# Input table of a state space branch with its powers and products in PSUM, and the output table issued beside it

## The chip, the cores and the metric

The kernel runs on one core of one Trainium2 chip. The core has a matrix engine (TensorE, PE in the profile), VectorE (DVE), ScalarE (ACT), GpSimd (POOL), and DMA queues that SyncE (SP) issues. Each engine takes its instructions in the order of the program and waits for the others by semaphores. SBUF is the working memory; PSUM has eight banks of 2 KB per partition, in which TensorE leaves its products. The metric is the device time of one execution in microseconds.

## The reference, cut to what matters

One layer of an encoder with two branches; the change is in branch A, a bidirectional state space layer with 32 groups of 64 complex states.

```python
def _s5_branch(u, lam_re, lam_im, log_step, b_re, b_im, c_re, c_im, d_skip):
    ...
        ab_re = mag * jnp.cos(li * dt)
        ab_im = mag * jnp.sin(li * dt)
        ...
        bu_re = jnp.einsum('blgh,gph->blgp', ug, bb_re)
        bu_im = jnp.einsum('blgh,gph->blgp', ug, bb_im)
        ...
        _, _, s_re, s_im = lax.associative_scan(
            _cplx_scan_combine, (a_re, a_im, bu_re, bu_im), reverse=(direction == 1), axis=1)
        y = (y + jnp.einsum('blgp,ghp->blgh', s_re, c_re[direction].astype(f32))
             - jnp.einsum('blgp,ghp->blgh', s_im, c_im[direction].astype(f32)))
```

## The kernel before, in words

The sequence is cut into chunks of 8 positions. Powers 0 to 8 of the complex state factor (`pw`, made by `s5_params`) turn the branch into matrix products. An input table E (powers `pwE` times the input weights `Bb`) takes the 8 positions of a chunk to the state that the chunk adds; the products land in `X`. A scan over 64 chunk steps carries the state on, in place in `X`. An output table F (powers `pwF` times the output weights `Cc`) takes the carried state back to 8 positions; it is stored to DRAM (`fbscr`), and small kernels made of it (`kdscr`) are the part inside a chunk.

Both tables are made in 8 banks of 4 groups by `gbank`, six 128x512 operations a bank: on VectorE for E (`neg` false), on GpSimd for F (`neg` true). The rest of the stage is written as lanes, generators whose steps are issued at due times on a hand-kept clock of TensorE work: `e_lane` (E bank, its transposes on TensorE, the products with the input `Vt`, three copies to `X`, the last by VectorE), `scan_lane` ("r", 64 steps of three VectorE operations), `table_lane` ("s": F bank b, ScalarE's copies for it, TensorE's products of bank b-1 with `bm`, and for bank b-2 a VectorE addition to `ks` and the stores), `decay_params` ("d", VectorE), `ret_tables` ("x") and `y_lane` ("y", which reads both tables back and needs the whole scan). Between them run the plain projections (`kq_unit`, `v_unit`), whose weights are split into a high part `whi` by ScalarE and a low part `wlo` by VectorE.

The due times before start the table lane at 12 with a step of 5.4; the e lane runs from 0 to 12 and the scan starts at 13. Outside `gbank` the PSUM tiles are two-bank `pair` tiles (two of them) and one-bank `single` tiles (four of them). `late_params`, called near the end of the e lane, takes a `single` for the scan's factors (`A8`) and fills `pwF`.

An instruction that waits holds back all that stands behind it on its engine; so a `wlo` or a copy to `X` on VectorE stands behind whatever bank or scan step was issued before it. SP issues all DMAs in one order too: the store of F bank b-1 stands behind the `kdscr` stores of bank b-2, of which one waits for VectorE's addition to `ks`.

Of the kernel before, what the change touches and what calls it, by code (L numbers as in the profile page):

```python
# [8 lines left out]
F32 = mybir.dt.float32  # L9
# [42 lines left out]
R_T = (13, 0.997)  # L52
D_T = (15, 0.629)
X_T = (45, 1.361)
S_T = (12, 5.4)
T_FREE = 82.607
C_DT = 2.446
Y_T = (73, 3.91)
# [3 lines left out]
def build(nc, tc, I, O):  # L62
# [73 lines left out]
    def pair():  # L136
        return pp.tile([128, 2, 512], F32, name="pair", tag="pair")

    def single():
        return p1.tile([128, 512], F32, name="single", tag="single")  # L140
# [238 lines left out]
    prm = sp.tile([128, 3, G], F32, name="prm")  # L379
    Bb = sp.tile([128, 2, G, 16], F32, name="Bb")  # L380
    Cc = sp.tile([128, 2, G, 16], F32, name="Cc")
    pwE = sp.tile([128, 2, 8, G], F32, name="pwE")
    pwF = sp.tile([128, 2, 9, G], F32, name="pwF")
    Dg = sp.tile([48, 16, G], F32, name="Dg")

# [33 lines left out]
    def together(*gens):  # L419
        gens = list(gens)  # L420
        while gens:
            for g in list(gens):
                if next(g, gens) is gens:
                    gens.remove(g)
                else:
                    yield
# [4 lines left out]
            yield  # L431

    pw = sp.tile([128, 2, 9, G], F32, name="pw")
    sc = A8 = None

    def s5_params():
        V.memset(pw[:, 0, 0, :], 1.0)
        V.memset(pw[:, 1, 0, :], 0.0)
        dt = tmp()
        V.tensor_copy(out=dt, in_=prm[:, 2, :])  # L440
        yield
        yield from pexp(dt, G)
        lr, li = prm[:, 0, :], prm[:, 1, :]
        mag, den, dn = tmp(), tmp(), tmp()
        sc = []

        def magnitude():
            tt(V, mag, lr, dt, MUL)
            yield
            yield from pexp(mag, G)  # L450

        def angle():
            th, k1, kf, r, zz = tmp(), tmp(), tmp(), tmp(), tmp()
            c1 = 6.28125
            c2 = 0.0019340515136718750
            c3 = 2 * math.pi - c1 - c2
            yield from chain(
                lambda: tt(V, th, li, dt, MUL),
                lambda: ts(V, k1, th, 1.0 / (2 * math.pi), MUL, MAGIC, ADD),
                lambda: ts(V, kf, k1, -MAGIC, ADD),  # L460
                lambda: stt(r, kf, -c1, th, MUL, ADD),
                lambda: stt(r, kf, -c2, r, MUL, ADD),
                lambda: stt(r, kf, -c3, r, MUL, ADD),
                lambda: ts(V, r, r, 0.25, MUL),
                lambda: tt(V, zz, r, r, MUL))
            sn, cs = tmp(), tmp()

            def sine():
                ts(V, sn, zz, 1.0 / 362880, MUL)
                yield  # L470
                for c in (-1.0 / 5040, 1.0 / 120, -1.0 / 6):
                    stt(sn, sn, c, zz, ADD, MUL)
                    yield
                stt(sn, sn, 1.0, r, ADD, MUL)
                yield

            def cosine():
                ts(V, cs, zz, -1.0 / 3628800, MUL)
                yield
                for c in (1.0 / 40320, -1.0 / 720, 1.0 / 24, -0.5):  # L480
                    stt(cs, cs, c, zz, ADD, MUL)
                    yield
                ts(V, cs, cs, 1.0, ADD)
                yield

            yield from together(sine(), cosine())
            for _ in range(2):
                s2, c2t = tmp(), tmp()
                yield from chain(
                    lambda: tt(V, c2t, sn, sn, MUL),  # L490
                    lambda: stt(s2, sn, 2.0, cs, MUL, MUL),
                    lambda: ts(V, c2t, c2t, -2.0, MUL, 1.0, ADD))
                sn, cs = s2, c2t
            sc.extend((sn, cs))

        def denominator():
            yield from chain(
                lambda: tt(V, den, lr, lr, MUL),
                lambda: tt(V, dn, li, li, MUL),
                lambda: tt(V, den, den, dn, ADD),  # L500
                lambda: V.reciprocal(out=den, in_=den))

        yield from together(angle(), magnitude(), denominator())
        sn, cs = sc
        tt(V, pw[:, 0, 1, :], mag, cs, MUL)
        yield
        tt(V, pw[:, 1, 1, :], mag, sn, MUL)
        yield

        def powers():  # L510
            for st, n in ((1, 1), (2, 2), (4, 4)):
                ts_ = [x0.tile([128, 4, G], F32, name="pq", tag="pq", bufs=4)[:, :n] for _ in range(4)]
                ar = pw[:, 0, st:st + 1, :].to_broadcast([128, n, G])
                ai_ = pw[:, 1, st:st + 1, :].to_broadcast([128, n, G])
                xr, xi = pw[:, 0, 1:1 + n, :], pw[:, 1, 1:1 + n, :]
                for t, a, b in zip(ts_, (xr, xi, xr, xi), (ar, ai_, ai_, ar)):
                    tt(V, t, a, b, MUL)
                    yield
                tt(V, pw[:, 0, st + 1:st + 1 + n, :], ts_[0], ts_[1], SUB)
                yield  # L520
                tt(V, pw[:, 1, st + 1:st + 1 + n, :], ts_[2], ts_[3], ADD)
                yield

        bts = [x0.tile([128, G, 16], F32, name="bt", tag="bt", bufs=2) for _ in range(2)]

        def inputs():
            t1, t2, t3, t4, cr, ci, nr = (tmp() for _ in range(7))
            ai = pw[:, 1, 1, :]
            yield from chain(
                lambda: ts(V, nr, pw[:, 0, 1, :], -1.0, ADD),  # L530
                lambda: tt(V, t2, ai, li, MUL),
                lambda: tt(V, t3, ai, lr, MUL),
                lambda: tt(V, t1, nr, lr, MUL),
                lambda: tt(V, t4, nr, li, MUL),
                lambda: tt(V, t1, t1, t2, ADD),
                lambda: tt(V, t3, t3, t4, SUB),
                lambda: tt(V, cr, t1, den, MUL),
                lambda: tt(V, ci, t3, den, MUL))
            crb = cr[:, :, None].to_broadcast([128, G, 16])
            cib = ci[:, :, None].to_broadcast([128, G, 16])  # L540
            br, bi = braw[:, 0], braw[:, 1]
            tt(P, Bb[:, 0], br, crb, MUL)
            tt(P, bts[0], bi, cib, MUL)
            tt(P, Bb[:, 0], Bb[:, 0], bts[0], SUB)
            tt(V, Bb[:, 1], bi, crb, MUL)
            yield
            tt(V, bts[1], br, cib, MUL)
            yield
            tt(V, Bb[:, 1], Bb[:, 1], bts[1], ADD)
            yield  # L550

        yield from together(inputs(), powers())
        for ri in range(2):
            V.tensor_copy(out=pwE[0:64, ri], in_=pw[0:64, ri, 7::-1, :])
            yield
            V.tensor_copy(out=pwE[64:128, ri], in_=pw[64:128, ri, 0:8, :])
            yield

    def late_params():
        nonlocal sc, A8  # L560
        sc = single()
        A8 = sc[:, 0:128].rearrange("p (k r g) -> p k r g", k=2, r=2)
        for ri in range(2):
            V.tensor_copy(out=A8[:, 0, ri, :], in_=pw[:, 0, 8, :])
            ts(V, A8[:, 1, ri, :], pw[:, 1, 8, :], 1.0 if ri == 0 else -1.0, MUL)
            V.tensor_copy(out=pwF[0:64, ri, 1:9], in_=pw[0:64, ri, 1:9, :])
            V.tensor_copy(out=pwF[64:128, ri, 1:9], in_=pw[64:128, ri, 8:0:-1, :])  # L567
        ts(P, Cc[:, 1], Cc[:, 1], -1.0, MUL)
        tt(P, Dg[32:48], eye[32:48, :, None].to_broadcast([16, 16, G]),
           dcol[32:48, None, :].to_broadcast([16, 16, G]), MUL)  # L570

    x0_cm = pool("x0")
    x0 = enter(x0_cm)
# [177 lines left out]
    BK = 4  # L751
    NB = G // BK

    def gbank(b, pwt, t0, Bm, neg):
        gs = slice(b * BK, (b + 1) * BK)
        er9 = s5t.tile([128, BK, 9, 16], F32, name="er", tag="er", bufs=2)
        ei9 = s5t.tile([128, BK, 9, 16], F32, name="ei", tag="ei", bufs=2)
        er, ei = er9[:, :, 1:9], ei9[:, :, 1:9]
        if neg:
            act(er9[:, :, 0], Bm[:, 0, gs], AF.Copy)  # L760
# [3 lines left out]
        pi = pwt[:, 1, t0:t0 + 8, gs].rearrange("p t g -> p g t")[:, :, :, None].to_broadcast(sh)  # L764
        br = Bm[:, 0, gs, None, :].to_broadcast(sh)
        bi = Bm[:, 1, gs, None, :].to_broadcast(sh)
        tm = s5.tile([128, BK, 8, 16], F32, name="tm", tag="tm", bufs=1)
        tn = s5t.tile([128, BK, 8, 16], F32, name="tn", tag="tn", bufs=1)
        e = P if neg else V
        tt(e, er, pr, br, MUL)  # L770
        tt(e, tm, pi, bi, MUL)
# [298 lines left out]
    def spread(name, t0, dt, n):  # L1070
        return [(t0 + dt * i, name) for i in range(n)]

    events = deque(sorted(
        spread("e", *E_T, 16) + spread("r", *R_T, 64) + spread("s", *S_T, 10) + spread("d", *D_T, 45) + spread("x", *X_T, 24)
        + [(T_FREE, "free")] + spread("c", T_FREE + 0.1, C_DT, 12) + spread("y", *Y_T, 12), key=lambda e: e[0]))

    def passed(t):
# [1379 lines left out]
```

## Time and profile before

| | |
|---|---|
| median of 3 runs | 1308.06 us (1307.3 to 1308.17) |
| profiled execution | 1307.5 us, its span 1305.7 us |
| TensorE busy in the span | 1214.7 us (93%) |
| VectorE busy | 957.6 us (73%) |
| ScalarE busy | 591.7 us (45%) |
| GpSimd busy | 648.4 us (50%) |

The span is what the profile's clock covers; the execution's own time is 1.8 us longer. Times below are from the start of the span. The stage of the change lies between 56 us (the first E bank) and 226 us (the first products of the y lane). "Busy" is time in which an engine had an instruction running; an idle time in brackets stands before the instruction that ended it, with what released it. A row of busy times by stretch names the engines in the order TensorE, its weight loads, VectorE, ScalarE, GpSimd, with their instructions in brackets.

### The profile page before, as it was taken

How to read it: one execution, taken by the hardware profiler on the slowest of the kernel's cores; microseconds unless marked ns; L12 is line 12 of the kernel's file. 1: busy time of each engine (PE TensorE's matmuls, PEld its weight loads, DVE VectorE, ACT ScalarE, POOL GpSimd, SP SyncE). 2: the span in 40 equal slices, each digit the busy share in tenths (PEclk: the TensorE clock that was granted, in tenths of full speed). 3: DMA queues.
4: the chain of work that ended last, by engine and by line, in shares of the span. 5: the costliest groups of instructions: out<-in, count | busy, mean ns of one | idle time of the engine just before them, and what ended most of it. 6: DMA issues, size and time to landing. Idle time of an engine off the chain costs nothing. (4 is left out here: it accounts for less than half of the span.)

```text
span 1305.7 us, 19189 instructions
## 1 busy us (share of the span) xinstructions
PE 1214.7 (93%) x6821; PEld 1142.3 (87%) x6821; DVE 957.6 (73%) x1590; ACT 591.7 (45%) x1238; POOL 648.4 (50%) x621
## 2 busy tenths in 40 slices
PE   7899788998899999987899998999999999999996
PEld 7789678998888989976899887999999999988884
DVE  6997998548877776889764349856656556799797
ACT  5264344544354444342433224444444444567564
POOL 4306570436676656377755117543443444474174
PEclk8899889999999999997999999999999999999998
DMA  6351446766455433322353601333331222524002
GB/s 245 79 111 46 140 135 184 179 187 185 153 170 173 136 125 133 111 81 91 122 155 87 213 11 49 122 105 96 99 105 65 65 73 73 202 97 147 15 1 96
DMA packets 74495, 152.18 MB, mean 117 GB/s; under 512 B 17808, under 2 KB 35344, under 8 KB 74400
## 3 DMA queue, kind: packets, MB, share of 16 engines
q1 hardware_dynamic: 74400, 150.97, 37.5%
q8 instruction: 53, 0.87, 0.3%
q14 instruction: 42, 0.34, 0.1%
HBM read 116.92 MB, written 34.01 MB: 116 GB/s over the span
## 5 line engine op out<-in xcount | busy, mean ns | idle before, releaser
L90 DVE TENSOR_TENSOR wlo<-wraw,whi 128x512 fp32r<-128x512 f32 x298 | 246.7, 836 | 104.9 <-ACT whi L102 104.0
L102 ACT ACTIVATE whi<-wraw 128x512 fp32r<-128x512 f32 x304 | 183.3, 623 | 59.1 <-POOL wraw L90 32.8
L90 POOL TENSOR_TENSOR wraw<-wraw 128x512 f32<-128x512 f32 x93 | 132.1, 1421 | 139.5 <-DVE wlo L90 92.8
L90 POOL TENSOR_TENSOR wraw<-wrax,wraw 128x512 f32<-128x512 f32 x38 | 51.0, 1343 | 72.2 <-DVE wlo L90 41.3
L84 PE MATMUL bank<-n1hi,wlo 128*128 128x384 f32 x192 | 66.0, 344 | 1.7 <-DVE wlo L90 1.7
L82 PE MATMUL bank<-n1hi,whi 128*128 128x384 f32 x192 | 67.4, 351 | 0.0
L83 PE MATMUL bank<-n1lo,whi 128*128 128x384 f32 x192 | 66.0, 344 | 0.0
L82 PE MATMUL pair<-n1hi,whi 128*128 128x384 f32 (+1 forms) x168 | 62.2, 370 | 3.0 <-ACT sgst L102 3.0
L102 ACT ACTIVATE q<-bank 128x384 f32<-128x384 f32 x80 | 38.1, 483 | 52.8 <-PE bank L84 48.7
L84 PE MATMUL pair<-n1hi,wlo 128*128 128x384 f32 (+1 forms) x168 | 59.7, 355 | 0.0
L83 PE MATMUL pair<-n1lo,whi 128*128 128x384 f32 (+1 forms) x168 | 59.6, 355 | 0.0
L90 DVE TENSOR_TENSOR wlo<-wrax,whi 128x512 fp32r<-128x512 f32 x50 | 43.8, 883 | 15.8 <-ACT whi L102 15.8
L2289 PE MATMUL acc<-whi,ahi 128*128 128x512 f32 x132 | 52.4, 397 | 0.6 <-DVE hres L90 0.6
L2289 PE MATMUL acc<-whi,alo 128*128 128x512 f32 x132 | 52.3, 396 | 0.0
L2289 PE MATMUL acc<-wlo,ahi 128*128 128x512 f32 x132 | 52.3, 396 | 0.0
L90 DVE TENSOR_TENSOR X<-X,single 128x128 f32<-128x128 f32 (+2 forms) x128 | 42.9, 335 | 4.4
L90 POOL TENSOR_TENSOR er<-pwF,Cc 128x512 f32<-128x512 f32 x8 | 8.9, 1111 | 74.0 <-DVE pwF L567 43.0
L83 PE MATMUL bank<-yTlo,whi 128*128 128x384 f32 x128 | 43.0, 336 | 1.5 <-DVE yTlo L90 1.5
L84 PE MATMUL bank<-yThi,wlo 128*128 128x384 f32 x128 | 43.0, 336 | 0.8 <-DVE wlo L90 0.8
L82 PE MATMUL bank<-yThi,whi 128*128 128x384 f32 x128 | 42.9, 335 | 0.0
L82 PE MATMUL pair<-whi,n1hi 128*128 128x256 f32 x144 | 41.2, 286 | 0.0
L90 POOL TENSOR_TENSOR fr<-fr 128x384 f32<-128x384 f32 x29 | 36.6, 1275 | 8.8 <-DVE alo L90 8.2
(525 smaller groups left out, 4319.6 us busy)
## 6 DMA issues: line engine op xcount, KB each, us to landing
wraw<-in_wfi SPq DMA_DIRECT2D x35, 512.0 KB, 3.7
wraw<-in_win SPq DMA_DIRECT2D x33, 512.0 KB, 5.3
w<-in_wfo SPq DMA_DIRECT2D x16, 512.0 KB, 4.9
wrax<-in_win SPq DMA_DIRECT2D x11, 512.0 KB, 4.3
wrax<-in_wfi SPq DMA_DIRECT2D x11, 512.0 KB, 3.7
fb<-fbscr SPq DMA_DIRECT2D x8, 512.0 KB, 5.0
wraw<-in_wo SPq DMA_DIRECT2D x8, 512.0 KB, 3.6
ffscr<-fr SPq DMA_DIRECT2D x10, 384.0 KB, 2.9
```

The lines of the kernel that those rows point to most:

```text
L82: T.matmul(out, l[0], r[0], start=start, stop=False)
L83: T.matmul(out, l[0], r[1], start=False, stop=False)
L84: T.matmul(out, l[1], r[0], start=False, stop=stop)
L90: e.tensor_tensor(out=out, in0=a, in1=b, op=op)
L102: A.activation(out=out, in_=a, func=f, **kw)
L2289: T.matmul(ps, l[a], r[b], start=False, stop=False, skip_group_check=True)
```

## The change

`pwE` becomes a view of a PSUM tile (`sc`, a `single`), taken at the end of `s5_params` and kept until the scan has used it for `A8`. From bank 2 on, the two intermediate products of an E bank (`tm`, `tn`) lie in the two banks of one `pair` tile. `pwF` is filled at the end of `s5_params` too. The F banks get SBUF tiles of their own (`fr`, `fi`), and the table lane's due times become a list that starts at 0.8.

```diff
-S_T = (12, 5.4)
+S_T = (0.8, 3.1, 5.4, 7.7, 10, 12.3, 18, 24, 30, 36)
...
-    pwE = sp.tile([128, 2, 8, G], F32, name="pwE")
...
         yield from together(inputs(), powers())
+        nonlocal sc, pwE
+        sc = single()
+        pwE = sc.rearrange("p (r t g) -> p r t g", r=2, t=8)
         for ri in range(2):
             V.tensor_copy(out=pwE[0:64, ri], in_=pw[0:64, ri, 7::-1, :])
             yield
             V.tensor_copy(out=pwE[64:128, ri], in_=pw[64:128, ri, 0:8, :])
             yield
-
-    def late_params():
-        nonlocal sc, A8
-        sc = single()
-        A8 = sc[:, 0:128].rearrange("p (k r g) -> p k r g", k=2, r=2)
         for ri in range(2):
-            V.tensor_copy(out=A8[:, 0, ri, :], in_=pw[:, 0, 8, :])
-            ts(V, A8[:, 1, ri, :], pw[:, 1, 8, :], 1.0 if ri == 0 else -1.0, MUL)
             V.tensor_copy(out=pwF[0:64, ri, 1:9], in_=pw[0:64, ri, 1:9, :])
             V.tensor_copy(out=pwF[64:128, ri, 1:9], in_=pw[64:128, ri, 8:0:-1, :])
...
+    def late_params():
+        A8 = sc[:, 0:128].rearrange("p (k r g) -> p k r g", k=2, r=2)
+        for ri in range(2):
+            V.tensor_copy(out=A8[:, 0, ri, :], in_=pw[:, 0, 8, :])
+            ts(V, A8[:, 1, ri, :], pw[:, 1, 8, :], 1.0 if ri == 0 else -1.0, MUL)
...
-        er9 = s5t.tile([128, BK, 9, 16], F32, name="er", tag="er", bufs=2)
-        ei9 = s5t.tile([128, BK, 9, 16], F32, name="ei", tag="ei", bufs=2)
+        er9, ei9 = (s5t.tile([128, BK, 9, 16], F32, name=n, tag=n, bufs=2)
+                    for n in (("fr", "fi") if neg else ("er", "ei")))
...
-        tm = s5.tile([128, BK, 8, 16], F32, name="tm", tag="tm", bufs=1)
-        tn = s5t.tile([128, BK, 8, 16], F32, name="tn", tag="tn", bufs=1)
+        if b > 1 and not neg:
+            if not spare:
+                spare.append(pair())
+            tm, tn = (spare[0][:, i].rearrange("p (g t h) -> p g t h", g=BK, t=8) for i in range(2))
+        else:
+            tm = tn = s5.tile([128, BK, 8, 16], F32, name="tm", tag="tm", bufs=1)
```

On VectorE, between the last powers and the first E bank, before:

```order
L90 TENSOR_TENSOR pw<-pq 128x128 x2
L554 COPY pwE<-pw 64x256
L556 COPY pwE<-pw 64x256
L554 COPY pwE<-pw 64x256
L556 COPY pwE<-pw 64x256
L90 TENSOR_TENSOR er<-pwE,Bb 128x4x128
```

and in the changed program, where `single` is the PSUM tile `sc`:

```order
L90 TENSOR_TENSOR pw<-pq 128x128 x2
L556 COPY single<-pw 64x256
L558 COPY single<-pw 64x256
L556 COPY single<-pw 64x256
L558 COPY single<-pw 64x256
L561 COPY pwF<-pw 64x256
L562 COPY pwF<-pw 64x256
L561 COPY pwF<-pw 64x256
L562 COPY pwF<-pw 64x256
L90 TENSOR_TENSOR er<-single,Bb 128x4x128
```

Four copies that stood behind the last E bank now stand in front of the first.

On TensorE, in the e lane behind the second E products (`Vt` with `et`) and before the next projection, before; numbers tell the `single` tiles apart:

```order
L87 MATMUL single_899<-Vt_646,et_784 128x99 x4
L87 MATMUL single_907<-Vt_646,et_784 128x99 x4
L784 MATMUL single_926<-ident_77,er_842 128x128 x4
L784 MATMUL single_932<-ident_77,ei_843 128x128 x4
...
L87 MATMUL single_951<-Vt_646,et_852 128x99 x4
L87 MATMUL single_959<-Vt_646,et_852 128x99 x4
L784 MATMUL single_978<-ident_77,er_915 128x128 x4
L784 MATMUL single_984<-ident_77,ei_916 128x128 x4
```

and in the changed program:

```order
L87 MATMUL single_902<-Vt_652,et_788 128x99 x4
L87 MATMUL single_910<-Vt_652,et_788 128x99 x4
L791 MATMUL single_948<-ident_77,er_846 128x128 x4
L791 MATMUL single_954<-ident_77,ei_847 128x128 x4
...
L87 MATMUL single_981<-Vt_652,et_855 128x99 x4
L87 MATMUL single_1009<-fr_922,bm0_918 48x144
L87 MATMUL single_1009<-fi_923,bm0_918 48x144
L87 MATMUL single_1009<-fr_922,bm0_918 48x144
L87 MATMUL single_1009<-fi_923,bm0_918 48x144
L87 MATMUL single_1015<-fr_922,bm0_918 48x144
...
L791 MATMUL single_1030<-ident_77,er_939 128x128 x4
L791 MATMUL single_1036<-ident_77,ei_940 128x128 x4
```

The `single` tiles take turns in three PSUM banks instead of four while the e lane runs, so 954 takes the bank that 902 had (before, 951 took that of 899, twelve projection products later). Eight products of F bank 0 now stand between two E banks; three more such groups (banks 1 to 3) come before the last E products, where before all eight came after them.

## Rows read from the trace of the kernel before

**Rows 1.** Busy time by stretch: stretch, length, each engine (instructions), granted clock, DMA share, GB/s.

```profile
56.00:109.10 53.10, 46.94 (x308) 45.58 (x309) 43.29 (x83) 28.78 (x64) 9.30 (x10) 0.90 0.43 91
109.10:188.00 78.90, 66.89 (x359) 60.94 (x359) 75.25 (x172) 29.79 (x103) 46.90 (x40) 0.91 0.38 112
188.00:222.60 34.60, 32.45 (x248) 31.31 (x246) 31.93 (x92) 12.57 (x27) 6.58 (x6) 1.00 0.58 170
```

**Rows 2.** Timeline of VectorE: start, length, instruction, idle time before it.

```profile
56.24 0.69 DVE L90 TENSOR_TENSOR er<-pwE,Bb 128x512 f32<-128x512 f32 x1
...
69.77 2.50 DVE L90 TENSOR_TENSOR wlo<-wraw,whi 128x512 fp32r<-128x512 f32 x4 [0.17 <-ACT whi L102]
72.30 0.30 DVE L814 COPY X<-single 64x128 f32<-64x128 f32 x1
...
98.37 0.28 DVE L566 COPY pwF<-pw 64x256 f32<-64x256 f32 x1
...
109.14 0.40 DVE L90 TENSOR_TENSOR single<-X,single 64x128 f32<-64x128 f32 x1
...
221.94 0.58 DVE L90 TENSOR_TENSOR X<-X,single 128x64 f32<-128x64 f32 x2
```

**Rows 3.** Timeline of TensorE.

```profile
58.31 1.12 PE L784 MATMUL single<-ident,er 128*128 128x128 f32 x4 [4.29 <-DVE er L90]
...
72.22 0.60 PE L784 MATMUL single<-ident,ei 128*128 128x128 f32 x4
...
114.13 0.45 PE L87 MATMUL single<-er,bm 128*48 128x144 f32 x2
...
115.89 0.41 PE L87 MATMUL single<-ei,bm 128*48 128x144 f32 x2
...
223.11 0.46 PE L87 MATMUL single<-Vt,tg 128*128 128x97 f32 x2 [2.08 <-DMA tg<-kdscr]
```

**Rows 4.** TensorE's longest wait for GpSimd, 109 to 190 us: total, times, longest.

```profile
PE single L87 <- POOL ei L90: 7.5, 3, 3.1
```

**Rows 5.** VectorE's groups by form, 109.1 to 222.6 us: busy, mean ns, idle before.

```profile
L90 DVE TENSOR_TENSOR single<-X,single 128x256 f32<-128x256 f32 x31 | 19.6, 632 | 0.3
...
L90 DVE TENSOR_TENSOR wlo<-wraw,whi 128x512 fp32r<-128x512 f32 x12 | 9.6, 845 | 0.0
L99 DVE SCALAR_TENSOR_TENSOR pt<-pt,pt 128x8 f32<-128x8 f32 x17 | 7.7, 453 | 0.2
...
L94 DVE TENSOR_SCALAR dcols<-lgc 128x4 f32<-128x4 f32 x6 | 2.6, 465 | 0.0
L94 DVE TENSOR_SCALAR pt<-pt 128x8 f32<-128x8 f32 x4 | 2.3, 587 | 0.0
L90 DVE TENSOR_TENSOR wlo<-wrax,whi 128x512 fp32r<-128x512 f32 x2 | 2.1, 1100 | 0.0
L841 DVE COPY X<-X 64x64 f32<-64x64 f32 x1 | 1.2, 1161 | 0.0
...
L94 DVE TENSOR_SCALAR pt<-dlg 128x8 f32<-128x8 f32 x2 | 0.3, 160 | 0.0
...
L99 DVE SCALAR_TENSOR_TENSOR lgc<-pt,pt 128x8 f32<-128x8 f32 x1 | 0.2, 168 | 0.0
```

**Rows 6.** The same view, 56 to 109.1 us.

```profile
L90 DVE TENSOR_TENSOR wlo<-wraw,whi 128x512 fp32r<-128x512 f32 x6 | 3.8, 687 | 0.2 <-ACT whi L102 0.2
```

**Rows 7.** Timelines of VectorE and GpSimd around one pair of `wlo`.

```profile
147.27 2.21 DVE L90 TENSOR_TENSOR wlo<-wraw,whi 128x512 fp32r<-128x512 f32 x2
...
147.28 1.65 POOL L90 TENSOR_TENSOR tm<-pwF,Cc 128x512 f32<-128x512 f32 x1
```

**Rows 8.** TensorE's granted clock after its idle time (columns as in rows 1).

```profile
58.00:62.00 4.00, 2.87 (x11) 2.47 (x12) 3.96 (x8) 1.21 (x3) 0.00 (x0) 0.50 0.90 247
```

**Rows 9.** Timeline of VectorE: an operation with a PSUM input.

```profile
237.28 0.56 DVE L90 TENSOR_TENSOR gt<-single,gt 128x388 f32<-128x388 f32 x1
```

More of the change, by code (lines that the diff above doesn't have):

```diff
@@ L433, in build @@
     pw = sp.tile([128, 2, 9, G], F32, name="pw")
-    sc = A8 = None
+    sc = pwE = None
     def s5_params():
@@ L444, in s5_params @@
         mag, den, dn = tmp(), tmp(), tmp()
-        sc = []
+        sincos = []
         def magnitude():
@@ L493, in angle @@
                 sn, cs = s2, c2t
-            sc.extend((sn, cs))
+            sincos.extend((sn, cs))
         def denominator():
@@ L503, in s5_params @@
         yield from together(angle(), magnitude(), denominator())
-        sn, cs = sc
+        sn, cs = sincos
         tt(V, pw[:, 0, 1, :], mag, cs, MUL)
@@ L752, in build @@
     NB = G // BK
+    spare = []
     def gbank(b, pwt, t0, Bm, neg):
         gs = slice(b * BK, (b + 1) * BK)
-        er9 = s5t.tile([128, BK, 9, 16], F32, name="er", tag="er", bufs=2)
-        ei9 = s5t.tile([128, BK, 9, 16], F32, name="ei", tag="ei", bufs=2)
+        er9, ei9 = (s5t.tile([128, BK, 9, 16], F32, name=n, tag=n, bufs=2)
+                    for n in (("fr", "fi") if neg else ("er", "ei")))
         er, ei = er9[:, :, 1:9], ei9[:, :, 1:9]
@@ L1073, in build @@
     events = deque(sorted(
-        spread("e", *E_T, 16) + spread("r", *R_T, 64) + spread("s", *S_T, 10) + spread("d", *D_T, 45) + spread("x", *X_T, 24)
+        spread("e", *E_T, 16) + spread("r", *R_T, 64) + [(t, "s") for t in S_T] + spread("d", *D_T, 45) + spread("x", *X_T, 24)
         + [(T_FREE, "free")] + spread("c", T_FREE + 0.1, C_DT, 12) + spread("y", *Y_T, 12), key=lambda e: e[0]))
```

## The prediction

> **What bounds the kernel now.** I read the busy times by stretch first. From 56 to 109 us TensorE is busy for 46.9 of 53.1 us and VectorE for 43.3; from 109 to 188 us VectorE is busy for 75.3 of 78.9 us and TensorE for only 66.9 [rows 1]. So the stage has two parts with two bounds. The timeline of VectorE gives the border: the scan's first operation starts at 109.14 and its last ends at 222.5 [rows 2]. Since VectorE hardly idles in between, the length of the scan, 113.4 us, is the sum of what VectorE does there. On TensorE the first products of the y lane come right after, at 223.11 [rows 3]. The end of the stage is thus the start of the scan plus the scan's length on VectorE, and what happens later shifts with it one for one.
>
> The waits of TensorE look as if they pointed elsewhere: 7.5 us for GpSimd's `ei` in the table lane [rows 4]. They are no gain to be had. TensorE has 12.0 us without work in that stretch [rows 1] while VectorE has none to speak of; without these waits TensorE would wait for the scan instead.
>
> What is to be had is inside VectorE's own operations. The same `wlo` takes 687 ns each before the scan [rows 6] and 845 ns in it [rows 5]; an 8-element operation with three SBUF inputs takes 453 ns on average where one of its form took 168 [rows 5]. The two timelines show why: a pair of `wlo` at 147.27 took 2.21 us, and GpSimd's `tm` that began beside it 1.65 us [rows 7], against 1.17 us for GpSimd's mean operation in the stretch (46.9 us in 40 [rows 1]). The two engines alternate. The scan's own operations, which have one operand in PSUM, don't show it: the mean of 31 is 632 ns and the idle time before them 0.3 us in all [rows 5]. The Trainium skill ("SBUF — State Buffer", Who interferes with whom) calls the port pair that the two engines share an exclusive lock, taken by a VectorE operation with two SBUF inputs against a GpSimd operation that reads SBUF; these rows agree.
>
> How much this costs in the scan, from [rows 5] and the undisturbed `wlo` of [rows 6]: `wlo` from `wraw` 12 x (845 - 687) = 1.9 us; `wlo` from `wrax` 2 x (1100 - 687) = 0.8; the three-operand form 17 x (453 - 168) = 4.8; `dcols` 6 x (465 - 160) = 1.8; the scalar form on `pt` 4 x (587 - 160) = 1.7; the copy within `X` 1161 - 300 = 0.9 (a copy to `X` of twice as many elements took 0.30 [rows 2]). Sum 11.9 us.
>
> **The change, part by part.** It has two effects on the end: when the scan starts, and how long it takes.
>
> *Start of the E banks.* Four `pwF` copies now stand ahead of the first `er`. One took 0.28 us [rows 2], so 1.1 us; but the `pwE` copies beside them may be shorter than before, since none of them has to share with GpSimd when it writes PSUM, and the same four copies leave the stretch before the scan. TensorE's idle of 4.29 us before the first transposes [rows 3] grows by what is added. I take +0.5, bounds 0 and 1.2.
>
> *Four groups of F products before the last E products.* One group of eight lasts from 114.13 to the end of 115.89's last, 2.0 us [rows 3]. Before, all groups stand behind the last `Vt` products; now those of banks 0 to 3 stand ahead of them. TensorE is the fuller engine in that part, so the scan starts 4 x 2.0 = +8.0 us later. They could fill idle time instead, but of the 6.2 us that TensorE idles there [rows 1], 4.29 are the wait for the first bank [rows 3], in which no F product is ready. Bounds 6.1 (the other 1.9 us filled) and 8.0.
>
> *Three `single` banks instead of four.* The transposes of E bank 2 (`single` 954 in the order) need the bank that 902 had, and 902 is read last by VectorE's copy to `X`. Before, that copy ran at 72.30, behind four `wlo` of 2.50 us, and the transposes at 72.22 [rows 2, 3], in another bank. In the changed program the four `wlo` meet F bank 0 on GpSimd, which begins as soon as the copies to `pwF` and the SBUF buffer `tm`, which E banks 0 and 1 still use, allow. Four `wlo` with three GpSimd operations between them last 4 x 0.62 (a quarter of the 2.50) + 3 x 1.17 = 6.0 us instead of 2.5. The copy then ends at 72.6 + 0.5 + 3.5 = 76.6 and the transposes, due at 72.7, wait 3.9 us. Queued behind them on TensorE are the projections and the next E products, so the whole lane is late. I take +3.9; bounds 0.4 (no alternation yet) and 6 (GpSimd also comes between the copies).
>
> *Clock.* After the 4.29 us of idle at 54 to 58 us the granted clock was 0.50 from 58 to 62 us [rows 8], the lower level, which cost 2 of 4 us. A wait of 3.9 us could do the same in part. I take +1.3, bounds 0 and 3.
>
> *PSUM operands of the E banks.* From bank 2 on, none of the six operations of a bank has two SBUF inputs, so F banks beside them cost them nothing. Their own time: an operation with a PSUM input took 0.56 us for 388 elements [rows 9], an E operation in SBUF 0.69 for 512 [rows 2]: the same per element. I take 0; the upper bound is below, as a rival.
>
> Start of the scan: 0.5 + 8.0 + 3.9 + 1.3 = +13.7, that is at about 122.8.
>
> *The scan.* The lock's 11.9 us go where GpSimd is done. Its work in 109 to 188 us is 46.9 us [rows 1]. With two buffers for `fr` and `fi`, bank 6 waits for the products and the store of bank 4, whose due time is about the scan's start, so two banks stay in the scan: 12 x 1.17 = 14.1 us, 30%. Regained: 11.9 x 0.70 = 8.3 us. Bounds 5 (four banks stay) and 11.9.
>
> *Waits of TensorE for GpSimd* go, worth nothing (above): the cover is the scan on VectorE. If VectorE's part became so short that TensorE's 66.9 + 32.5 us [rows 1] counted, they would be worth up to 7.5; with four groups of F products moved ahead, 8.0 us, and 14.1 us without work there already [rows 1], TensorE has some 22 us of slack.
>
> Sum against the profiled execution of 1307.5 us, whose span is 1.8 us shorter (the median is 0.56 us above it, well inside the 2.6 us, 0.2%, that I take as the least that a measurement tells from no change): 13.7 - 8.3 = +5.4, 1312.9 us.
>
> **The rivals.**
>
> *The lock goes and the stall doesn't come: faster.* If the four `wlo` are through before F bank 0 begins, term three is 0.4, the clock's 0; if the F groups fill 1.9 us of idle, the start shifts by 0.5 + 6.1 + 0.4 = 7.0 us, and with F banks 6 and 7 over early the scan is shorter by 11.9: 1307.5 - 4.9 = 1302.6. For it: GpSimd was busy for only 9.3 of 53.1 us before the scan [rows 1], so there is room for five banks of 6 x 1.17 = 7.0 us. Against it: the third bank is really gone, and bank 0 on GpSimd is due with the first E banks. The point that decides is whether VectorE's copy behind the four `wlo` ends before TensorE reaches the bank. If it does so with 8.3 us regained, the end is 1307.5 + 7.0 - 8.3 = 1306.2.
>
> *A wash.* The stall doesn't come, but the groups cost their 8.0: 0.5 + 8.0 + 0.4 - 8.3 = +0.6, 1308.1.
>
> *PSUM operands are slow.* The scan's operations with a PSUM operand rise by 632 ns for 256 elements [rows 5] against 0.40 for 128 [rows 2], about 1.8 ns an element. If that were PSUM's doing and not that of the scan's layout, an E operation would take 0.69 + 0.36 = 1.05 us, 36 of them 13 us more. VectorE's 43.3 + 13.0 = 56.3 us would exceed the 53.1 us [rows 1], and the start would slip by some 8 us more: 1321. Against it stands the 0.56 us of [rows 9]. The Trainium skill ("VectorE: DVE Perf Modes", The TRN2 errata) gives a PSUM source 62 cycles more of fixed time than an SBUF source, which by its clock is an estimate of 65 ns, some 2.3 us for the 36; no row here shows that.
>
> **How the numbers follow.** The forecast (a full stall, two banks left) 0.47, with its own range 1308 to 1318 from the bounds of its terms; the faster rival, in either of its sizes, 0.28; the wash 0.15; slow PSUM operands 0.10. Faster by over 2.6 us: 0.25 of the faster rival and 0.06 of the wash and the forecast's lower edge, 0.31. Within: 0.03, 0.10 of the wash, and 0.07 of the forecast, 0.20. Slower: the rest, 0.49. The range reaches from just below the faster rival, 1302, to 1319; beyond lie most of slow operands and a little of the faster side.
>
> **What the profile after would show.** Right: the scan's first operation at 119 to 125 us and its last at 226 to 229; a wait of TensorE for VectorE's copy to `X` at the transposes near 73 to 77 us; four `wlo` near 70 us that take about 6 us; the three-operand form on `pt` well below 453 ns; TensorE's waits for GpSimd's `ei` gone; E operations at 0.69 us. Wrong: a scan that starts before 117 us (the groups filled idle time or the stall didn't come), E operations of 1 us (PSUM is slow), or a three-operand form still near 450 ns (GpSimd's banks still meet it), which would take away what is regained and make it slower than the forecast.

## The result, and the profile after

The changed kernel takes 1316.41 us (median of 4 runs, 1313.02 to 1317.68) against 1307.68 of the kernel before (4 runs): a ratio of 1.0069, 95% interval 1.0054 to 1.0085, so 8.7 us slower. The profiled execution took 1317.68 us with a span of 1315.6; it is the slowest of the four, so the two profiles, which the readings below compare, are 10.2 us apart and not 8.7.

The prediction cut the stage at the scan's first and last operation on VectorE. The same two places after, with the operations that mattered on the way (timeline of VectorE, columns as in [rows 2]):

```profile
71.13 6.28 DVE L90 TENSOR_TENSOR wlo<-wraw,whi 128x512 fp32r<-128x512 f32 x4 [0.59 <-ACT whi L102]
...
77.44 0.50 DVE L821 COPY X<-single 64x128 f32<-64x128 f32 x2
77.98 0.69 DVE L90 TENSOR_TENSOR er<-single,Bb 128x512 f32<-128x512 f32 x1
...
125.11 0.39 DVE L90 TENSOR_TENSOR single<-X,single 64x128 f32<-64x128 f32 x1
...
230.99 0.58 DVE L90 TENSOR_TENSOR X<-X,single 128x64 f32<-128x64 f32 x2
```

The scan starts 16.0 us later than in [rows 2] (125.11 - 109.14) and ends 9.05 us later (231.57 - 222.52): it is 106.5 us long instead of 113.4. What happens after it shifts along: the first products of the y lane, which start at 223.11 in [rows 3] (and not at 226, as is said ahead of the rows), start at 232.30. TensorE's timeline (columns as in [rows 3]):

```profile
59.16 1.12 PE L791 MATMUL single<-ident,er 128*128 128x128 f32 x4 [5.71 <-DVE er L90]
...
73.64 0.60 PE L791 MATMUL single<-ident,er 128*128 128x128 f32 x4
77.80 1.11 PE L791 MATMUL single<-ident,ei 128*128 128x128 f32 x4 [3.56 <-DVE X L821]
82.55 2.33 PE L87 MATMUL single<-Vt,et 128*128 128x99 f32 x16
84.81 0.45 PE L87 MATMUL single<-fr,bm 128*48 128x144 f32 x2
...
86.90 0.66 PE L791 MATMUL single<-ident,er 128*128 128x128 f32 x4
...
232.30 0.46 PE L87 MATMUL single<-Vt,tg 128*128 128x97 f32 x2 [1.74 <-DMA tg<-kdscr]
```

The same instructions in the timeline of before:

```profile
71.78 0.60 PE L784 MATMUL single<-ident,er 128*128 128x128 f32 x4
...
74.77 1.92 PE L87 MATMUL single<-Vt,et 128*128 128x99 f32 x16
76.53 0.60 PE L784 MATMUL single<-ident,er 128*128 128x128 f32 x4
```

Read against these and [rows 3], this gives the 16.0 us piece by piece. The first transposes are 0.85 us late (59.16, was 58.31). The third transposes' first half is 1.86 us late (73.64, was 71.78). Their second half waits 3.56 us for VectorE's copy to `X`, the wait that the prediction placed there. The products behind it are 7.8 us late (82.55, was 74.77), so the wait and the time after it cost 5.9 us; the products themselves take 0.5 us longer to the next instruction (84.81 - 82.55, was 76.53 - 74.77). From 84.81 to 86.90 stands a group of F products, 2.1 us, the first of four: 8.4 us. These pieces make 16.7; smaller differences that go both ways take off the other 0.7.

Where the 5.9 us and the 0.5 us went is in the busy times by stretch (columns as in [rows 1]): TensorE has 0.44 us of work in four, and then works at a granted clock of 0.50, the lower of its two levels, for four more.

```profile
74.00:78.00 4.00, 0.44 (x4) 0.21 (x2) 3.94 (x6) 3.04 (x11) 3.92 (x3) 0.82 1.28 119
78.00:82.00 4.00, 4.00 (x15) 4.00 (x15) 3.86 (x6) 0.60 (x1) 2.74 (x3) 0.50 1.20 211
82.00:86.00 4.00, 4.00 (x29) 3.90 (x28) 0.45 (x2) 2.40 (x6) 0.00 (x0) 0.83 0.91 320
```

GpSimd's timeline beside the four `wlo`: its operations, 1.11 to 1.3 us when alone, take 1.55 there, and the `wlo` 6.28 us instead of 2.50.

```profile
66.16 1.12 POOL L90 TENSOR_TENSOR tm<-pwF,Cc 128x512 f32<-128x512 f32 x1 [9.23 <-DVE ei L90]
...
72.13 1.55 POOL L90 TENSOR_TENSOR fr<-pwF,Cc 128x512 f32<-128x512 f32 x1
73.65 1.55 POOL L90 TENSOR_TENSOR tm<-pwF,Cc 128x512 f32<-128x512 f32 x1
75.27 1.59 POOL L90 TENSOR_TENSOR fr<-fr,tm 128x512 f32<-128x512 f32 x1
```

What the scan gave back, in the busy times of exactly the scan, first of before and then of after:

```profile
109.14:222.52 113.38, 99.31 (x605) 92.21 (x603) 107.15 (x261) 42.27 (x129) 53.45 (x45) 0.94 0.44 130
```

```profile
125.11:231.57 106.46, 87.17 (x537) 83.60 (x534) 100.32 (x257) 30.97 (x79) 21.67 (x18) 0.94 0.37 116
```

VectorE is busy for 6.8 us less, which is the scan's gain of 6.9; GpSimd's work in it fell from 53.5 to 21.7 us. By group (125 to 231.6 us, columns as in [rows 5]):

```profile
L90 DVE TENSOR_TENSOR wlo<-wraw,whi 128x512 fp32r<-128x512 f32 x12 | 10.4, 904 | 0.0
L99 DVE SCALAR_TENSOR_TENSOR pt<-pt,pt 128x8 f32<-128x8 f32 x17 | 6.9, 406 | 0.3
...
L90 DVE TENSOR_TENSOR rt<-rt 128x512 f32<-128x512 f32 x3 | 2.1, 693 | 0.1
L90 DVE TENSOR_TENSOR ks<-ks,Dg 16x64 f32<-16x64 f32 x5 | 1.8, 362 | 0.2
L90 DVE TENSOR_TENSOR wlo<-wrax,whi 128x512 fp32r<-128x512 f32 x2 | 1.3, 690 | 0.0
...
L94 DVE TENSOR_SCALAR dcols<-lgc 128x4 f32<-128x4 f32 x6 | 0.8, 160 | 0.0
L94 DVE TENSOR_SCALAR pt<-pt 128x8 f32<-128x8 f32 x4 | 0.6, 160 | 0.0
...
L848 DVE COPY X<-X 64x64 f32<-64x64 f32 x1 | 0.2, 221 | 0.0
```

Two groups of before that [rows 5] doesn't show:

```profile
L90 DVE TENSOR_TENSOR ks<-ks,Dg 16x64 f32<-16x64 f32 x8 | 3.1, 390 | 0.2
L90 DVE TENSOR_TENSOR rt<-rt 128x512 f32<-128x512 f32 x3 | 3.0, 1016 | 0.1
```

`dcols`, the scalar form on `pt`, `wrax` and the copy are at their undisturbed length; the three-operand form still meets GpSimd (453 to 406 ns), and `wlo` went up from 845 to 904. Of the eight `ks` additions four have left the scan (the first of the five shown stands just ahead of it, at 124.82), and `rt` has its undisturbed length too.

### The profile page after: what moved, and what is told of

It is laid out like the page before. It is cut to its first block, busy times and chain, and to the rows that moved or that the text cites. A ratio compares the mean times of both kernels' runs of the same rounds, so it can differ in the third digit from the quotient of the medians.

```text
span 1315.6 us, 19179 instructions
## 1 busy us (share of the span) xinstructions
PE 1213.7 (92%) x6821; PEld 1142.9 (87%) x6821; DVE 959.8 (73%) x1590; ACT 591.6 (45%) x1238; POOL 649.2 (49%) x621
## 5 line engine op out<-in xcount | busy, mean ns | idle before, releaser
L90 DVE TENSOR_TENSOR wlo<-wraw,whi 128x512 fp32r<-128x512 f32 x298 | 254.0, 861 | 105.9 <-ACT whi L102 105.6
L82 PE MATMUL pair<-n1hi,whi 128*128 128x384 f32 (+1 forms) x168 | 62.4, 371 | 18.5 <-ACT sgst L102 18.3
L90 DVE TENSOR_TENSOR wlo<-wrax,whi 128x512 fp32r<-128x512 f32 x50 | 43.9, 885 | 16.7 <-ACT whi L102 16.7
L82 PEld LDWEIGHTS pair<-n1hi,whi 128*128 128x128 f32 x168 | 34.0, 203 | 21.2 <-ACT sgst L102 19.9
L90 POOL TENSOR_TENSOR sx<-n1hi,sy 128x384 f32<-128x384 f32 x4 | 4.7, 1172 | 96.1 <-DVE n1t5lo L90 96.1
```

The source lines that it names most:

```text
L82: T.matmul(out, l[0], r[0], start=start, stop=False)
L90: e.tensor_tensor(out=out, in0=a, in1=b, op=op)
```

## The experiments

Start, end and length of the scan are read from the profile of each kernel as above; the ratio is to the kernel before, run on the same chip in turn; for the changed kernel that was 1307.68 us. A profile is of one execution, up to 3.6 us from the kernel's median (decay_early, 1313.24 us). Behind the scan the thirteen profiled executions take another 1079.9 to 1085.1 us of their spans, so where the scan ends in one profile doesn't give the median to better than some 2 us.

| kernel | scan from | to | length | median us | ratio, 95% interval |
|---|---|---|---|---|---|
| before | 109.1 | 222.5 | 113.4 | 1306.5 to 1306.8 | 1 |
| changed | 125.1 | 231.6 | 106.5 | 1316.41 | 1.0069 (1.0054 to 1.0085) |
| late_list | 116.3 | 228.3 | 112.1 | 1311.54 | 1.0041 (1.0027 to 1.0055) |
| x_act | 117.9 | 224.3 | 106.3 | 1309.30 | 1.0021 (1.0011 to 1.0031) |
| late_x_act | 110.9 | 224.4 | 113.5 | 1308.70 | 1.0018 (1.0006 to 1.0029) |
| psum_only | 108.9 | 222.2 | 113.2 | 1306.53 | 1.0002 (0.9993 to 1.0012) |
| f_cut_before | 109.0 | 212.8 | 103.8 | 1297.30 | 0.9926 (0.9914 to 0.9938) |
| f_cut_after | 117.1 | 217.9 | 100.8 | 1303.23 | 0.9977 (0.9967 to 0.9986) |
| decay_psum | 108.6 | 218.8 | 110.2 | 1300.78 | 0.9955 (0.9942 to 0.9967) |
| x_act_decay | 116.7 | 223.9 | 107.2 | 1308.10 | 1.0009 (1.0000 to 1.0018) |
| decay_early | 121.6 | 226.6 | 105.0 | 1309.65 | 1.0026 (1.0015 to 1.0036) |
| x_act_early | 127.8 | 227.1 | 99.4 | 1312.92 | 1.0045 (1.0030 to 1.0059) |
| two_groups | 125.4 | 226.7 | 101.3 | 1311.87 | 1.0041 (1.0026 to 1.0056) |

**late_list**: the changed kernel with the old due times.

```diff
-S_T = (0.8, 3.1, 5.4, 7.7, 10, 12.3, 18, 24, 30, 36)
+S_T = tuple(12 + 5.4 * i for i in range(10))
```

> The changed kernel with the table lane's old due times (12, then every 5.4): the PSUM tiles, the early copies of pwF and the F bank's own buffers stay, but no group of F products stands before the last E products. GpSimd can still make banks 0 and 1 early, since only its buffers hold it. Theory (the four groups lengthen TensorE's part before the scan, and the stall of the transposes behind VectorE's copy to X is separate): the scan starts 8.4 us earlier than in the changed kernel, at about 117, the wait of about 3.6 us for the copy stays, and some 3 to 4 us of what the scan regained are lost again; about 1312 us. Rival (the groups only fill time in which TensorE idles): the start stays near 125 and the time rises to about 1320.

The start moved by 8.9 us, the time to 1311.5; the rival (the groups only fill idle time) falls. The wait stays, on the same instruction:

```profile
78.42 1.11 PE L791 MATMUL single<-ident,ei 128*128 128x128 f32 x4 [3.30 <-DVE X L821]
```

The scan lost more than expected, 5.6 us. The kernel before had F bank 0 and two of the six operations of bank 1 done before its scan too (its GpSimd starts at 99), so making both banks early takes only 4.4 us of GpSimd work out of the scan: 49.1 of 53.5 us are left in it.

**x_act**: the changed kernel with the last copy to `X` on ScalarE.

```diff
-                V.tensor_copy(out=X[64:128, :, gs, 67:99], in_=psv[64:128, :, :, 98:66:-1])
+                act(X[64:128, :, gs, 67:99], psv[64:128, :, :, 98:66:-1], AF.Copy)
```

> The changed kernel with the last of the copies to X made by ScalarE instead of VectorE, so that no PSUM bank of the E products is given back by VectorE. Theory (VectorE's copy, queued behind four wlo that alternate with GpSimd, stalls the third transposes, and the idle time costs TensorE's clock): the wait of 3.6 us and the 2.2 us at the lower clock go, the scan starts at about 119.5; about 1311 us. Rival (the transposes are then held by something else that is as late): no change, about 1316 us.

The start came down by 7.2 us with the scan's length unchanged, and the time to 1309.3, 1.7 us less than expected. The four `wlo` still take 6.14 us, but nothing on TensorE waits for what stands behind them: in 74 to 82 us TensorE is busy for 7.35 us at full clock.

```profile
71.14 6.14 DVE L90 TENSOR_TENSOR wlo<-wraw,whi 128x512 fp32r<-128x512 f32 x4 [0.77 <-ACT whi L102]
```

```profile
74.00:82.00 8.00, 7.35 (x55) 6.74 (x53) 7.93 (x11) 7.74 (x29) 6.50 (x5) 1.00 1.13 158
```

**late_x_act**: both edits.

> Both edits together: old due times and the copy to X by ScalarE. Theory: the two costs add up, so both go; the scan starts at about 111, banks 0 and 1 of F are out of the scan; about 1306 us, at or a little below the kernel before. Rival (the groups are free, only the stall costs): about 1314 us.

The start is 110.9 as expected, but the scan is as long as before, so the time is 1308.7, not 1306. Beside x_act it shows the price of the four groups: the start 7.0 us later, the scan 7.1 us shorter, the times 0.6 us apart with overlapping intervals. Bringing F products ahead is a wash by itself here.

**psum_only**: old due times, and the `pwF` copies back in `late_params`.

> Only the PSUM tiles of the changed kernel: old due times, and the copies to pwF late as before, so that GpSimd has nothing to do beside the E banks. Theory (three single banks stall only where VectorE's wlo alternate with GpSimd; PSUM operands cost VectorE nothing): the four wlo take 2.5 us, the third transposes wait for at most 0.5 us, E operations take 0.69 us, the scan starts at 109 to 110.5 and is 113.4 us long; about 1308 us. Rival (PSUM tiles are a cost by themselves, by the third bank or by slow operands): 1312 us or more.

As expected: the `wlo` take 2.50 us, the third transposes don't wait, E operations take 0.69 us, the scan runs from 108.9 to 222.2, and the time can't be told from before. The PSUM tiles and the three banks cost nothing that these runs can tell (at most 0.12% by the interval) without GpSimd beside them.

**f_cut_before** and **f_cut_after**: in both kernels GpSimd makes only the first product of each half of an F bank and leaves out the second products and their additions, so the F table is incomplete.

```diff
         tt(e, er, pr, br, MUL)
-        tt(e, tm, pi, bi, MUL)
-        tt(e, er, er, tm, ADD if neg else SUB)
         tt(e, ei, pr, bi, MUL)
-        tt(e, tn, pi, br, MUL)
-        tt(e, ei, ei, tn, SUB if neg else ADD)
+        if not neg:
+            tt(e, tm, pi, bi, MUL)
+            tt(e, er, er, tm, SUB)
+            tt(e, tn, pi, br, MUL)
+            tt(e, ei, ei, tn, ADD)
```

> The kernel before with four of the six GpSimd operations of each F bank left out (both intermediate products and the additions of them), so that the F table lacks its second products; all else is unchanged. Theory (GpSimd's operations that read SBUF and VectorE's operations that read only SBUF exclude each other, and that lengthens the scan): with a third of the GpSimd work left, two thirds of 11.9 us go, the scan starts at 109 as before and is about 105.5 us long; about 1300 us. Rival (the small VectorE operations are long for a reason of their own): 113 us and about 1307 us.

> The changed kernel with the same four operations of each F bank left out. Theory: what is left of F banks 0 and 1 is done before the four wlo near 70 us, which take 2.5 us again; the wait for VectorE's copy (3.56 us) and the lower clock behind it go, the scan starts at about 119.5, since the four groups of F products (8.4 us) stay, and is about 104 us long; about 1307 us. Rival (the third transposes wait for the bank for another reason than GpSimd's work): the wait stays and the scan starts at 124 or later.

With less GpSimd work the scan of before falls by 9.6 us to 103.8, though VectorE has the same operations, and the three-operand form to 190 ns:

```profile
L99 DVE SCALAR_TENSOR_TENSOR pt<-pt,pt 128x8 f32<-128x8 f32 x17 | 3.2, 190 | 0.2
```

In the changed kernel the `wlo` are back at 2.49 us and the wait at 0.38, at the same instructions; the start is 117.1, 8 us later than before and in f_cut_before (109.0), which is what the four groups cost.

```profile
71.07 2.49 DVE L90 TENSOR_TENSOR wlo<-wraw,whi 128x512 fp32r<-128x512 f32 x4
```

```profile
73.94 0.66 PE L792 MATMUL single<-ident,ei 128*128 128x128 f32 x4 [0.38 <-DVE X L822]
```

Both beat their expectation by 2.7 and 3.8 us.

**decay_psum** (from the kernel before) and **x_act_decay** (from x_act): seven of the values of `decay_params` lie in free columns of `sc`, so that all but a few of its operations have one PSUM operand.

```diff
+    def ptmp(n):
+        if not cols:
+            return tmp(n)
+        c = cols.pop(0)
+        return sc[:, c:c + n]
...
-        k1, kf, r, p = tmp(n), tmp(n), tmp(n), tmp(n)
+        k1, kf, r, p = ptmp(n), ptmp(n), tmp(n), ptmp(n)
...
-        e, nx = tmp(8), tmp(8)
+        cols.extend(range(384, 512, 8))
+        e, nx, lgc = tmp(8), ptmp(8), ptmp(8)
...
-        z, zz, s, l = tmp(8), tmp(8), tmp(8), tmp(8)
+        z, zb, zz, s, l = ptmp(8), tmp(8), tmp(8), ptmp(8), tmp(8)
```

> The kernel before with one change of another kind: the small operations of decay_params that run among the scan steps keep one operand each in free columns of the PSUM tile sc, GpSimd's banks stay where they were. Theory (an operation with a PSUM operand doesn't share with GpSimd): the three-operand form falls from 453 to about 170 ns, the scalar forms from 465 and 587 to about 160 to 200; the scan starts at 109 and is about 106 us long, if TensorE's own work and its 9.5 us of waits for GpSimd allow it; about 1300 us, and at the most 1304 where TensorE becomes the bound. Rival (PSUM operands don't help): 1307 us.

> The changed kernel with the copy to X by ScalarE, as run before (scan from 117.9, 106.3 us long, 1309.3 us), and with the small operations of decay_params in PSUM. Theory: 5 us more of the scan go, to about 101.5 us; about 1304 us. Rival (what is left of the scan is not held by GpSimd): no change against 1309 us.

decay_psum is faster than both kernels: 1300.78 us, 0.45% below before. The operations fell as expected:

```profile
L99 DVE SCALAR_TENSOR_TENSOR single<-single,pt 128x8 f32<-128x8 f32 x15 | 2.6, 173 | 0.5
...
L94 DVE TENSOR_SCALAR dcols<-single 128x4 f32<-128x4 f32 x6 | 0.7, 150 | 0.0
```

But the scan fell by only 3.2 us instead of 7, and in x_act_decay not at all (1308.1 us, where 1304 was expected and 1309 was the rival's). The reason is in the timelines at an undisturbed pair, first of before and then of decay_psum:

```profile
125.37 0.84 DVE L90 TENSOR_TENSOR X<-X,single 128x128 f32<-128x128 f32 x2
126.12 0.36 DVE L99 SCALAR_TENSOR_TENSOR pt<-pt,pt 128x8 f32<-128x8 f32 x2
126.40 0.64 DVE L90 TENSOR_TENSOR single<-X,single 128x256 f32<-128x256 f32 x1
```

```profile
125.21 0.83 DVE L90 TENSOR_TENSOR X<-X,single 128x128 f32<-128x128 f32 x2
126.07 0.38 DVE L99 SCALAR_TENSOR_TENSOR single<-single,pt 128x8 f32<-128x8 f32 x2
126.49 0.62 DVE L90 TENSOR_TENSOR single<-X,single 128x256 f32<-128x256 f32 x1
```

In SBUF the pair overlaps its neighbours at both ends, and the scan's operations stand 1.03 us apart; with a PSUM operand there is a gap at both ends and they stand 1.28 us apart, 0.12 us more for each of the two. Of the 37 VectorE operations of `decay_params` 34 have a PSUM operand, so this would be about 4.1 us, an estimate from this one place. It fits the sum: the 37 operations are 8.8 us shorter, VectorE waits 0.9 us for ScalarE's `whi` ahead of the `wrax` pair, which it didn't before, other operations are 0.6 us longer, and the scan is 3.2 us shorter, which leaves 4.1. In x_act_decay there is the same wait of 0.9 us. Of decay_psum's 6.0 us, 3.8 lie before the scan's end; where the rest comes from is not settled, since what stands behind the scan varies by as much from kernel to kernel without an edit there.

**decay_early**, **x_act_early**, **two_groups**: the same operations moved beside the E banks.

```diff
-D_T = (15, 0.629)
+D_T = (1.5, 0.23)
```

two_groups also has `S_T = (0.8, 3.1, 5.4, 14, 19.4, 24.8, 30.2, 35.6, 41, 46.4)`.

> The kernel before with only the due times of decay_params moved from among the scan steps (15, then every 0.629) to beside the E banks (1.5, then every 0.23), where GpSimd is idle. Theory (these operations are long because GpSimd's F banks stand beside them in the scan): some 9 us leave VectorE's scan and 4 to 5 us go into a stretch in which VectorE has room; the scan starts at 109 to 111 and is about 105 us long; TensorE, with 99.3 us of work and 9.5 us of waits for GpSimd in that time, may then hold the y lane; 1298 to 1302 us. Rival (the operations are as costly to TensorE beside the E banks): the scan starts 5 us or more later and the time is 1304 or more.

> The changed kernel with the copy to X by ScalarE and the same early due times of decay_params, where now GpSimd's banks 0 to 4 stand too. Theory: the start moves from 117.9 by 0 to 3 us, since some of the operations meet GpSimd there, and the scan is about 100 us long; about 1303 us. Rival: what meets GpSimd holds the E banks, and the time stays at 1308 or more.

> As x_act_early, with two groups of F products before the last E products instead of four (due times 0.8, 3.1, 5.4, then 14 and every 5.4). Theory (a group costs 2.1 us of TensorE before the scan and gives back less than that where the decay operations are out of the scan): the scan starts 4 us earlier than in x_act_early and is 2 to 3 us longer; about 1302 us. Rival (a group gives back 2 us or more): 1304 us or more.

All three missed. The scan became as short as expected (105.0, 99.4 and 101.3 us), but it starts 12.4, 9.8 and 7.5 us later than in the kernel before, in x_act and in x_act respectively, and not 0 to 3. One reason isn't the cost of these operations at all: the first of the moved operations reads `dlg`, whose load lands only at about 80 us, and VectorE stands idle for it, for 7.04 us in decay_early and for 4.46 and 4.05 us in the other two. The next E bank stands behind it, so TensorE waits in turn and then has the lower clock; of decay_early:

```profile
80.63 0.17 DVE L94 TENSOR_SCALAR pt<-dlg 128x8 f32<-128x8 f32 x1 [7.04 <-DMA dlg<-in_dlg]
```

```profile
82.87 1.08 PE L784 MATMUL single<-ident,er 128*128 128x128 f32 x4 [5.87 <-DVE er L90]
```

```profile
80.00:84.00 4.00, 1.08 (x4) 0.71 (x4) 3.30 (x7) 0.00 (x0) 0.00 (x0) 0.50 0.71 258
84.00:88.00 4.00, 3.20 (x11) 3.21 (x12) 3.73 (x13) 1.19 (x2) 0.00 (x0) 0.50 0.01 2
```

At the first transposes of the bank after this one decay_early is 9.6 us behind the kernel before (91.37, was 81.82), so most of its 12.4 us is there right behind the late load. Between the same places x_act_early falls only 3.2 us behind x_act (90.34, was 87.10); there the moved operations also meet GpSimd (six of the three-operand form take 4.36 us from 89.28 on, and five 3.75 from 102.98 on). What these operations cost beside the E banks with `dlg` loaded in time and no GpSimd beside them stays untested.

Two groups instead of four changed the start by -2.3 us and the scan by +1.9: a wash once more.

## Why the prediction was right, and where its sizes were off

The direction, the place of the end and the three costs at the start held; the rule for what the scan gets back didn't. 1312.9 us was forecast (+5.4 against the profiled execution); +8.7 us was measured, inside the range. Three of the signs that the prediction named for being right were missed: the scan starts at 125.1 (119 to 125 was named), ends at 231.6 (226 to 229), and the three-operand form is at 406 ns and not well below 453.

- *Start of the E banks*, +0.5: measured +0.85, and a further 1.0 by 73.6 us. The last `pwF` copy, at 55.98, took 1.10 us, its twin at 55.36 only 0.29: GpSimd's first operation of F bank 0 had begun at 55.73.
- *Four groups of F products*, +8.0: by its own row (115.89 + 0.41 - 114.13) a group lasts 2.17 us and not 2.0. Measured: 8.4 in the profile, 8.9 when late_list takes them away, 7.0 between x_act and late_x_act, 8 left over in f_cut_after. That they would fill idle time is refuted.
- *Three banks*, +3.9: a wait of 3.56 us on the instruction that was named, gone when either VectorE leaves the chain (x_act) or GpSimd leaves the `wlo` alone (f_cut_after, psum_only). With the *clock*, +1.3, the term was 5.2; measured 6.4 by the rows (5.9 and the 0.5 behind it), 7.2 by x_act. With the wait at 3.56, 2.8 us are left for the clock, whose term was too small.
- *PSUM operands*, 0: E operations stay at 0.69 us, and psum_only is even with before. The rival of slow operands falls for these 512-element operations. (Its 0.36 us isn't what its own slope gives: 1.8 ns for each of 512 elements and the 0.17 us that are left of the 0.40 make 1.10 us, 0.41 more than 0.69.) The fixed time by which the Trainium skill ("VectorE: DVE Perf Modes", The TRN2 errata) has a PSUM source cost more than an SBUF source doesn't show here: the operation at 77.98 is as long as that in [rows 2]. For 8-element operations the gaps above point the way that the Trainium skill has it, at 0.12 us an operation by about twice the 65 ns that the prediction estimated from its figure.
- *What the scan gets back*, -8.3: measured -6.9, and even that by luck in part. The six groups of which the 11.9 us were made gave back only 5.4: the three-operand form 0.8 (17 x (453 - 406)), `dcols` 1.8, the scalar form 1.7, `wrax` 0.8, the copy 0.9, and `wlo` -0.7. The rest came from operations outside that sum: four `ks` additions that left the scan (1.6) and `rt` without GpSimd beside it (1.3 with its `rel` form), less 1.5 net for other small operations on `pt`, of which some now stand beside F bank 6. With the start's 16.0 for 13.7 this is what was mis-sized. The step that failed is that the 11.9 us go in proportion to GpSimd's work ("11.9 x 0.70"): with the 21.7 of 53.5 us that stayed, proportion gives 7.1. It matters which operations the work stands beside. Banks 6 and 7 stayed in the scan as said, but bank 7 stands just where the three-operand chain runs, and behind it come GpSimd's sums of `n1hi` and `n1lo`, earlier than before; together they kept 4.0 of that form's 4.8 us (17 x (406 - 168)). Two pairs of `wlo` met bank 6 (2.20 us) and the end of bank 7 with the sums (3.04), where an undisturbed pair takes 1.29; before, three pairs were hit, but less (2.21, 1.48 and 2.10). The timelines of GpSimd and VectorE in the scan:

```profile
128.55 1.11 POOL L90 TENSOR_TENSOR fr<-pwF,Cc 128x512 f32<-128x512 f32 x1 [2.31 <-ACT sgst L102]
...
143.28 1.12 POOL L90 TENSOR_TENSOR fr<-pwF,Cc 128x512 f32<-128x512 f32 x1 [6.80 <-DMA fbscr<-fr]
...
150.29 1.45 POOL L90 TENSOR_TENSOR sy<-n1hi,n1lo 128x384 f32<-128x384 f32 x1
```

```profile
129.60 2.20 DVE L90 TENSOR_TENSOR wlo<-wraw,whi 128x512 fp32r<-128x512 f32 x2
...
143.51 1.97 DVE L99 SCALAR_TENSOR_TENSOR pt<-pt,pt 128x8 f32<-128x8 f32 x2
...
149.25 3.04 DVE L90 TENSOR_TENSOR wlo<-wraw,whi 128x512 fp32r<-128x512 f32 x2
```

- *The exclusion of VectorE and GpSimd* was read from two rows; f_cut_before shows it by its effect: the same VectorE operations, 9.6 us less; and f_cut_after for the four `wlo`, 2.49 us instead of 6.28.
- *TensorE's waits for GpSimd worth nothing*: they are gone after (TensorE has no wait for `fr` or `fi` in the scan; it waits 18.3 us for ScalarE to write `sgst` there instead), and in every kernel of the table the first products of the y lane start 0.6 to 1.1 us behind the scan's last operation. So the end did follow VectorE's scan.

The faster rival needed the stall not to come and the groups to fill idle time; x_act made the first true, which brought 6 to 7 us, and is still 0.2% slower than before, since the second isn't so.

## What to carry to other kernels

Work that is moved from a full engine's stretch into an earlier one is only free if the earlier one has room on every engine that it touches: here the output table left VectorE's scan, but its products went to TensorE where that was the fuller engine, and each group cost what it gave back. Look at the inputs too: an operation that is issued before its input has landed holds back all that stands behind it on its engine (the 7.04 us for `dlg`). When GpSimd is set beside VectorE, look for the VectorE operations with only SBUF operands and for who stands behind them, a PSUM bank's last reader above all: the wait that cost most was TensorE's, for a copy of VectorE's that reads nothing of what was moved. Keeping the small operations' operands out of the shared way, where GpSimd already stands (decay_psum), did more than moving GpSimd's work.

## What the runs showed of the hardware

- A wait of 3.56 us on TensorE cost 6.4 us: the granted clock was 0.50 in the stretch from 78 to 82 us behind it and 0.83 in the next, and 0.50 behind the 5.87 us in decay_early too.
- A single 8-element VectorE operation of the three-operand form beside GpSimd's banks can take as long as a whole GpSimd operation (up to 1106 ns, median 167, in the kernel before), so its cost depends more on when it is issued than on its size.
- Short VectorE operations in SBUF overlap their neighbours in the scan by some 0.1 us at each end; with a PSUM operand they don't, at 0.12 us an operation (read at one pair, and in keeping with the length of decay_psum's scan).
